# Attention weights split early and kept as fp16 in DRAM: a one-core Trainium2 decoder trunk

## The chip, the cores and the metric

The kernel runs on one core of a Trainium2 chip. The core has four compute engines: TensorE (PE, matrix products; PEld is its loading of weights), VectorE (DVE), ScalarE (ACT) and GpSimd (POOL). SyncE (SP) issues DMAs, as POOL and ACT also can. Each engine works through its own queue of instructions in the order in which the program was built, and waits at an instruction until the semaphores named there are reached. The metric is the device time of one execution in microseconds (us). Before the change it was 1152.69 us, the median of three runs (1151.28 to 1153.98).

## The reference: what is computed

The input x is 512 tokens of width 1024 in float32. Layer 0 is a gated short convolution and an MLP; then one shared key and value side is projected; layer 1 is native sparse attention (compressed, selected and window branches, 16 heads) and an MLP; a last RMS norm follows. Cut to what matters here:

```python
def short_conv_mixer(h, w_in, conv_w, w_out):
    b_gate, c_gate, u = jnp.split(h @ w_in, 3, axis=-1)
    v = c_gate * u
    vp = jnp.pad(v, ((0, 0), (CONV_WIDTH - 1, 0), (0, 0)))
    conv = sum(conv_w[k] * vp[:, k:k + S] for k in range(CONV_WIDTH))
    return (b_gate * conv) @ w_out

def squared_relu_mlp(h, w1, w2):           # 1024 -> 4096 -> 1024
    return jnp.square(jax.nn.relu(h @ w1)) @ w2

# layer 0:  x += short_conv_mixer(rms(x), ...);  x += squared_relu_mlp(rms(x), w1[0], w2[0])
# then:     kv = rms(x) @ w_kv   (six parts of 256); compress_blocks(k), compress_blocks(v)
#           with phi_k_w1, phi_k_w2, phi_v_w1, phi_v_w2
# layer 1:  q, gates = rms(x) @ b_w_qg;  o = three branches of attention;  x += o @ b_w_o
#           x += squared_relu_mlp(rms(x), w1[1], w2[1])
```

All weights arrive in float32.

## The kernel before

**Precision by splitting.** TensorE multiplies in fp16. A float32 operand is split into a high part (rounded to fp16) and a low part (the remainder, fp16), and a product of two operands is three matmuls: high by high, high by low, low by high (`mm3`, L338 to L341). The high part of a weight is made by ACT (L193), the low part by DVE (L194), which reads the float32 weight and the high part.

**The weight pieces.** All weights are listed in `pieces` in the order of their use. A usual piece is 128 x 1024 float32, 512 KB: half of the 1024 rows (4 blocks of 128) by 256 columns. A piece goes through three steps. `load_piece` brings it into one of three `wst` buffers by a DMA on SP's queue. `convert_piece` splits it into one of four `whi` and one of four `wlo` buffers (L193, L194). `next_piece` hands it to the matmuls. `ahead` converts two pieces ahead of use, `drain(ahead())` does it at once, and after a conversion the next loads are issued. Which of the four buffers a piece gets, and where an instruction stands in its engine's queue, is decided when the program is built, by a list scheduler of the framework.

**The stages**, with their times in the profile: the first stage, where the input projection a_w_in is multiplied pair by pair (0 to 140 us; pair 0 to 47); the mixer's output projection a_w_out (140 to 181); layer 0's MLP in two halves, each of 8 up pairs and then a down projection (up 181 to 266, down 266 to 345, up 345 to 424, down 424 to 503); the lead-in of attention with the first key and value parts (503 to 559); attention (559 to 797); layer 1's MLP (797 to the end). A "pair" is two blocks of 128 output features; it takes two pieces and 48 matmuls of 512 columns.

**One up pair** (`mlp_up`): 48 matmuls; then ml_t on DVE (L497, relu and scale, two instructions), ml_z on ACT (L499, the square), four sums of ml_z on POOL (L501, for the down projection, which is done in seven products of half-size blocks), rh on ACT (L502, high part), rl on DVE (L503, low part). The conversions of the next two pieces (L193, L194) stand in the same ACT and DVE queues. ml_t has one buffer, ml_z two. The down projections take rh and rl of all 8 pairs of the half (L548 to L550) and weights that are first summed on DVE (L180) and then split (L182, L183), with buffers of their own.

**Attention** uses 26 usual pieces and two small ones (phi_k_w2, phi_v_w2): parts of w_kv (4), phi_k_w1 (4), phi_v_w1 (4), parts of b_w_qg (6), and b_w_o (8). It interleaves many small tasks of softmax and selection with their conversions, which are done there in steps, mostly of 512 columns.

Of the kernel before, what the change touches and what calls it, by code (L numbers as in the profile page):

```python
# [22 lines left out]
SW = 256.0  # L23
# [25 lines left out]
def body(ctx, tc, x, rel_bias, norm_mix, norm_mlp, mlp_w1, mlp_w2, a_w_in, a_conv_w, a_w_out,  # L49
# [42 lines left out]
    def mlp_pieces(layer):  # L92

        for half in range(2):
            for p in range(8 * half, 8 * half + 8):
                up_pair(mlp_w1[layer], p)
            for p in range(4):
                down_blocks(mlp_w2[layer], p, half)

# [2 lines left out]
            cols(w, c0, 256, scale, k, 4)  # L102


    v = a_w_in[0].rearrange("(c p) (s n) -> c p s n", p=128, s=3)
    for c in range(8):
        pieces.append((v[c, :, :, 0:256], (3, 256), SW))
    for p in range(1, 4):
        for part in (1, 2, 0):
            block(a_w_in[0], part * D + p * 256)  # L110
    for p in range(4):
        block(a_w_out[0], p * 256)
    mlp_pieces(0)
    for part in (2, 4, 3, 5):
        block(w_kv, part * 256)
    cols(b_w_qg[0], 1024, 48, SW)
    block(b_w_qg[0], 0)
    block(w_kv, 0)
    block(b_w_qg[0], 256)
    block(phi_k_w1, 0, SW, 0, 16)  # L120
# [6 lines left out]
    for g in range(0, 4, 2):  # L127
        for p in range(4):
            cols(b_w_o[0], p * 256, 256, SW, 2 * g, 4)
    mlp_pieces(1)  # L130

    NS, NW, AHEAD, PIECE = 3, 4, 2, 1024
# [14 lines left out]
    def load_piece():  # L147
        i = pos["dma"]
        if i >= len(pieces):
            return  # L150
        src, shape, _ = pieces[i]
        if shape is None:
            t = wk[0].tile([128, PIECE2], F32, name="wst2", bufs=NS2)
            for k, u in enumerate(src):
                nc.sync.dma_start(t[:, k * PIECE:k * PIECE + 512].rearrange("p (j n) -> p j n", j=2), u)
        else:
            t = wpool.tile([128, PIECE], F32, name="wst", bufs=NS)
            a, n = shape
            v = t[:, :a * n].rearrange("p (a n) -> p a n", a=a)
            if len(src.shape) == 4:  # L160
                v = v.rearrange("p a (j n) -> p a j n", j=2)
                for j in range(2):
                    nc.sync.dma_start(v[:, :, j], src[:, :, j])
            else:
                nc.sync.dma_start(v, src)
        staged[i] = t
        pos["dma"] += 1

    def convert_piece(step=1024):

        i = pos["cv"]
        if i >= len(pieces):
            return
        _, shape, sc = pieces[i]
        t = staged.pop(i)
        pos["cv"] += 1
        if shape is None:
            b = t.rearrange("p (k b n) -> p k b n", k=2, n=128)
            for e, o, x, y in W_SUMS:
                DVE.tensor_tensor(b[:, :, o], b[:, :, x], b[:, :, y], op=e)  # L180
            hi, lo = (wk[0].tile([128, 2, 7, 128], F16, name=n, bufs=NW2) for n in ("whi2", "wlo2"))
            ACT.activation(hi, b[:, :, 1:], AF.Copy, scale=sc)  # L182
            DVE.scalar_tensor_tensor(lo, b[:, :, 1:], sc, hi, op0=OP.mult, op1=OP.subtract)  # L183
            ready[i] = (hi, lo)
            yield
        else:
            a, n = shape
            hi = wpool.tile([128, PIECE], F16, name="whi", bufs=NW)
            lo = wpool.tile([128, PIECE], F16, name="wlo", bufs=NW)
            for s in range(0, a * n, step):  # L190
                e = min(s + step, a * n)
                w = t[:, s:e]
                ACT.activation(hi[:, s:e], w, AF.Copy, scale=sc)  # L193
                DVE.scalar_tensor_tensor(lo[:, s:e], w, sc, hi[:, s:e], op0=OP.mult, op1=OP.subtract)  # L194
                yield
            r = lambda w: w[:, :a * n].rearrange("p (a n) -> p a n", a=a)
            ready[i] = (r(hi), r(lo))
        while pos["dma"] < len(pieces):
            like = [j for j in range(pos["cv"], pos["dma"]) if blocked(j) == blocked(pos["dma"])]
            if len(like) >= (NS2 if blocked(pos["dma"]) else NS):  # L200
                break
            load_piece()

    def next_piece():

# [183 lines left out]
    for p in range(4):  # L389
# [42 lines left out]
        for dst in (pc, pu, pb):  # L432
            if p:
                dst += [acc(), acc()]
                pair(xs, dst)
            else:
                for k in range(2):
                    first_pairs(dst, ws[k], 6 + k)
            drain(ahead())
            for m in range(2):  # L440
                ch = 2 * p + m
                if dst is pc:
                    if m == 0:
# [27 lines left out]
    for p in range(4):  # L471
        po = [acc(), acc()]
        pair(ys, po)
        if p < 3:
            drain(ahead())
        for m in range(2):
            residual_in(po[m], 2 * p + m, 1.0 / (SY * SW))
            ss.add(X[:, 2 * p + m])
        for m in range(2):
            split_gain(xs, 2 * p + m, X[:, 2 * p + m], "mlp0")  # L480
        drain(ahead())
    first.__exit__(None, None, None)


    def mlp_up(xs, ss, rh, half, rb):
        turn[0] = 1
        for p in range(8):
# [3 lines left out]
            if first:  # L491
                pr = broadcast_rows(ss.r)
                rb = row_tile(pr, math.sqrt(SR) / (SW * SX))
            drain(ahead())
            t = wk[0].tile([128, 2, S], F32, name="ml_t", bufs=1)
            for m in range(2):
                DVE.scalar_tensor_tensor(t[:, m], ph[m], 0.0, rb, op0=OP.max, op1=OP.mult)  # L497
# [741 lines left out]
```

## Time and profile before

| | |
|---|---|
| median of three runs | 1152.69 us |
| the profiled execution, its own time | 1151.28 us |
| its span in the trace | 1149.5 us |
| TensorE busy | 1106.0 us |
| VectorE busy | 837.8 us |
| ScalarE busy | 582.7 us |
| GpSimd busy | 162.2 us |
| DMA, moved in all | 115.76 MB, mean 101 GB/s |
| granted TensorE clock | 0.994 |
| L193 (high parts) | 171 instructions, 142.2 us |
| L194 (low parts) | 171 instructions, 168.1 us |

An instruction's row in the timeline gives its start in us from the start of the span, its duration, engine, line, operation and output<-inputs with sizes; "x2" at its end means that two were joined; in brackets stand the idle time of the engine before it and what ended that idle time. A row of the DMA issues gives the transfer, the queue (SPq, POOLq, ACTq), the count, the size of each and the median time from issue to landing. A row of the chain of waits gives start, duration, engine, tile and line of a step of the chain that ended last.

### The profile page before, as it was taken

The numbers are of one execution on the slowest core, as the hardware profiler recorded it, in microseconds if no ns is written. First come the engines' busy times: TensorE is split into PE (matmuls) and PEld (weight loads), VectorE is DVE, ScalarE is ACT, GpSimd is POOL, SyncE is SP. The second block draws the span as 40 slices with busy tenths as digits, with TensorE's granted clock in tenths as the row PEclk, the third lists the DMA queues.
The fourth block names the chain that finished last, engine by engine and source line by source line (L and its number), as shares of the span: only waits on it lengthen the run. The fifth ranks groups of instructions, "written<-read, shape, count | busy, mean of one in ns | idle before, by whom it ended". The sixth has DMA issues, their size and how long they took to land.

```text
span 1149.5 us, 20386 instructions
## 1 busy us (share of the span) xinstructions
PE 1106.0 (96%) x7959; PEld 694.1 (60%) x7959; DVE 837.8 (73%) x1604; ACT 582.7 (51%) x983; POOL 162.2 (14%) x211
## 2 busy tenths in 40 slices
PE   9999999999999999999999899999999999999996
PEld 4444444447884458868466665765444688445885
DVE  4755557765897557988487898997985588754795
ACT  4523235345333444457679778676644534343452
POOL 0000000422000220000120023111132200022031
PEclk9999999999999999999999999999999999999998
DMA  6433235433433333314333530111643343330231
GB/s 208 130 92 110 92 111 174 119 93 93 127 98 108 109 110 107 97 55 122 110 79 99 143 94 19 57 38 38 186 126 99 88 126 110 104 99 19 75 92 74
DMA packets 149379, 115.76 MB, mean 101 GB/s; under 512 B 8612, under 2 KB 146564, under 8 KB 149284
## 3 DMA queue, kind: packets, MB, share of 16 engines
q1 hardware_dynamic: 146736, 109.47, 31.8%
q10 hardware_dynamic: 2260, 4.40, 1.3%
q8 instruction: 62, 1.02, 0.4%
q0 software_dynamic: 288, 0.61, 0.2%
q14 instruction: 33, 0.27, 0.1%
HBM read 110.22 MB, written 2.14 MB: 98 GB/s over the span
## 4 chain that ended last, share of the span: by engine, by line
PE 49%; DVE 20%; ACT 12%; issue 8%; POOL 6%; DMA 4%; SPq 0%; DVEq 0%; ACTq 0%; POOLq 0%
POOL ml_z L501 6%; PE a L340 4%; PE a L339 4%; PE a L341 4%; DVE wlo L183 4%; DMA wst<-mlp_w_dram 4%; ACT rh L502 3%; PE b L339 3%; PE b L340 3%; PE b L341 3%; PE c L341 3%; PE c L339 3%; PE c L340 3%; DVE wst L180 3%; DVE wlo L194 3%
## 5 line engine op out<-in xcount | busy, mean ns | idle before, releaser
L193 ACT ACTIVATE whi<-wst 128x1024 f16<-128x1024 f32 (+2 forms) x171 | 142.2, 857 | 128.3 <-PE b L340 40.0
L194 DVE SCALAR_TENSOR_TENSOR wlo<-wst,whi 128x1024 f16<-128x1024 f32 (+2 forms) x171 | 168.1, 990 | 47.3 <-ACT whi L193 47.1
L501 POOL TENSOR_TENSOR ml_z<-ml_z 128x256 f32<-128x256 f32 x128 | 101.1, 811 | 604.5 <-ACT ml_z L499 403.9
L182 ACT ACTIVATE whi<-wst 128x1792 f16<-128x1792 f32 x64 | 107.0, 1692 | 132.6 <-DVE wst L180 107.8
L341 PEld LDWEIGHTS <-wlo 128*128 128x128 f16 x1024 | 100.1, 98 | 109.3 <-DVE wlo L194 0.7
L339 PEld LDWEIGHTS <-whi 128*128 128x128 f16 x1024 | 100.4, 98 | 108.1 <-issue 3.7
L503 DVE TENSOR_TENSOR rl<-ml_z,rh 128x1792 f16<-128x1792 f32 x32 | 64.8, 2025 | 136.9 <-ACT rh L502 136.9
L340 PEld LDWEIGHTS <-whi 128*128 128x128 f16 x1024 | 100.2, 98 | 105.0 <-issue 1.7
L183 DVE SCALAR_TENSOR_TENSOR wlo<-wst,whi 128x1792 f16<-128x1792 f32 x64 | 129.8, 2033 | 3.6 <-ACT whi L182 3.6
L180 DVE TENSOR_TENSOR wst<-wst 128x256 f32<-128x256 f32 x256 | 105.9, 455 | 24.1 <-DMA wst<-mlp_w_dram 23.1
L502 ACT ACTIVATE rh<-ml_z 128x1792 f16<-128x1792 f32 x32 | 54.3, 1697 | 103.4 <-POOL ml_z L501 103.4
L550 PEld LDWEIGHTS <-wlo 128*128 128x128 f16 x896 | 88.1, 98 | 16.6 <-issue 5.1
L549 PEld LDWEIGHTS <-whi 128*128 128x128 f16 x896 | 88.1, 98 | 14.8 <-issue 3.9
L548 PEld LDWEIGHTS <-whi 128*128 128x128 f16 x896 | 88.2, 98 | 11.0
L499 ACT ACTIVATE ml_z<-ml_t 128x1024 f32<-128x1024 f32 x32 | 33.8, 1057 | 90.5 <-DVE ml_t L497 90.5
L341 PE MATMUL b<-xsh,wlo 128*128 128x512 f16 x208 | 78.8, 379 | 0.0
L340 PE MATMUL b<-xsl,whi 128*128 128x512 f16 x208 | 78.8, 379 | 0.0
L339 PE MATMUL b<-xsh,whi 128*128 128x512 f16 x208 | 78.7, 379 | 0.0
L922 ACT ACTIVATE at_p<-at_s,at_m 128x128 f32<-128x128 f32 (+3 forms) x128 | 71.3, 557 | 13.4 <-DVE at_m L919 13.0
L549 PE MATMUL a<-rl,whi 128*128 128x256 f16 x256 | 70.3, 275 | 4.6 <-DVE rl L503 4.6
L339 PE MATMUL c<-xsh,whi 128*128 128x512 f16 x192 | 72.8, 379 | 0.0
L340 PE MATMUL c<-xsl,whi 128*128 128x512 f16 x192 | 72.8, 379 | 0.0
(312 smaller groups left out, 2757.5 us busy)
## 6 DMA issues: line engine op xcount, KB each, us to landing
wst<-mlp_w_dram SPq DMA_DIRECT2D x256, 256.0 KB, 3.4
wst<-a_w_in_dram SPq DMA_DIRECT2D x18, 512.0 KB, 3.6
wst<-w_kv_dram SPq DMA_DIRECT2D x12, 512.0 KB, 3.7
T<-ext_d ACTq DMA_DIRECT2D x4, 1056.0 KB, 6.0
wst<-a_w_out_dram SPq DMA_DIRECT2D x8, 512.0 KB, 3.5
wst<-b_w_qg_dram SPq DMA_DIRECT2D x8, 512.0 KB, 4.3
wst<-b_w_o_dram SPq DMA_DIRECT2D x8, 512.0 KB, 3.5
wst<-a_w_in_dram SPq DMA_DIRECT2D x8, 384.0 KB, 5.5
```

Source lines behind the costliest of these rows:

```text
L180: DVE.tensor_tensor(b[:, :, o], b[:, :, x], b[:, :, y], op=e)
L182: ACT.activation(hi, b[:, :, 1:], AF.Copy, scale=sc)
L183: DVE.scalar_tensor_tensor(lo, b[:, :, 1:], sc, hi, op0=OP.mult, op1=OP.subtract)
L193: ACT.activation(hi[:, s:e], w, AF.Copy, scale=sc)
L194: DVE.scalar_tensor_tensor(lo[:, s:e], w, sc, hi[:, s:e], op0=OP.mult, op1=OP.subtract)
L339: PE.matmul(ps, w[0], xs[0], start=start, stop=False)
L340: PE.matmul(ps, w[0], xs[1], start=False, stop=False)
L341: PE.matmul(ps, w[1], xs[0], start=False, stop=stop)
L501: POOL.tensor_tensor(z[:, o], z[:, a], z[:, b], op=e)
L502: ACT.activation(rh[0][:, p], z[:, 1:8], AF.Copy)
L548: PE.matmul(acc7[i], wh, xh, start=c == 0 and not other, stop=False, skip_group_check=other)
L549: PE.matmul(acc7[i], wh, xl, start=False, stop=False, skip_group_check=other)
```

## The change

Of attention's 28 pieces, the 26 of full size are taken out of attention's conversions. Behind each part of pairs 1 to 3 of the first stage (9), each pair of a_w_out (4) and the first 13 up pairs of layer 0 (8 in the first half, 5 in the second), one of them is added to the list of pieces (`spare_piece`). It goes through load and conversion like any other, in the same rings of three `wst` and four `whi` and `wlo` buffers. When its turn comes, `store_piece` takes it and writes its two fp16 parts to DRAM (`kept`), by two DMAs of 256 KB on GpSimd's queue; then it converts ahead as usual. In attention the piece is loaded by two DMAs on SP's queue directly into a `whi` and a `wlo` buffer, and not converted. The two small pieces are treated as before. In the program built, L193 and L194 with 171 instructions each become 147 each; GpSimd issues 58 DMAs in place of 6, and SP 415 in place of 363. The matmuls are the same.

```diff
         for half in range(2):
             for p in range(8 * half, 8 * half + 8):
                 up_pair(mlp_w1[layer], p)
+                if layer == 0:
+                    spare_piece()
...
+    late = pieces[:]
+    pieces.clear()
+    spare = [k for k, (_, shape, _) in enumerate(late) if shape[0] * shape[1] == 1024]
+    stores, loads, kept = {}, {}, {}
+
+    def spare_piece():
+        if spare:
+            stores[len(pieces)] = spare[0]
+            pieces.append(late[spare.pop(0)])
...
+    for p in range(1, 4):
+        for part in (1, 2, 0):
+            block(a_w_in[0], part * D + p * 256)
+            spare_piece()
+    for p in range(4):
+        block(a_w_out[0], p * 256)
+        spare_piece()
+    mlp_pieces(0)
...
+    for k, (src, shape, sc) in enumerate(late):
+        if shape[0] * shape[1] == 1024:
+            loads[len(pieces)] = k
+        pieces.append((src, shape, sc))
...
-        if shape is None:
+        if i in loads:
+            t = []
+            for name, d in zip(("whi", "wlo"), kept[loads[i]]):
+                w = wpool.tile([128, PIECE], F16, name=name, bufs=NW)
+                nc.sync.dma_start(w, d)
+                t.append(w.rearrange("p (a n) -> p a n", a=shape[0]))
+        elif shape is None:
...
-        if shape is None:
+        if i in loads:
+            ready[i] = tuple(t)
+        elif shape is None:
...
+            if i in loads:
+                full = i >= pos["use"] + NW - 1
+            else:
+                like = [j for j in range(pos["cv"], i) if j not in loads and blocked(j) == blocked(i)]
+                full = len(like) >= (NS2 if blocked(i) else NS)
+            if full:
+                break
             load_piece()
+
+    def store_piece():
+        i = pos["use"]
+        if i not in stores:
+            return
+        kept[stores[i]] = [dram.tile([128, PIECE], F16, name=f"kept{i}{m}") for m in "hl"]
+        for d, w in zip(kept[stores[i]], next_piece()):
+            nc.gpsimd.dma_start(d, w.rearrange("p a n -> p (a n)"))
+        drain(ahead())
...
         drain(ahead())
+        store_piece()
...
             drain(ahead())
+            store_piece()
             t = wk[0].tile([128, 2, S], F32, name="ml_t", bufs=1)
```

More of the change, by code (lines that the diff above doesn't have):

```diff
@@ L102, in block @@
             cols(w, c0, 256, scale, k, 4)
[L105 to L117, printed above, removed]
     block(w_kv, 0)
@@ L129, in body @@
             cols(b_w_o[0], p * 256, 256, SW, 2 * g, 4)
+    late = pieces[:]
[6 more added lines that the diff above has]
+            pieces.append(late[spare.pop(0)])
+    v = a_w_in[0].rearrange("(c p) (s n) -> c p s n", p=128, s=3)
+    for c in range(8):
+        pieces.append((v[c, :, :, 0:256], (3, 256), SW))
+    for p in range(1, 4):
[6 more added lines that the diff above has]
+    mlp_pieces(0)
+    for part in (2, 4, 3, 5):
+        block(w_kv, part * 256)
+    cols(b_w_qg[0], 1024, 48, SW)
+    block(b_w_qg[0], 0)
+    for k, (src, shape, sc) in enumerate(late):
+        if shape[0] * shape[1] == 1024:
+            loads[len(pieces)] = k
+        pieces.append((src, shape, sc))
+    assert not spare
     mlp_pieces(1)
@@ L198, in convert_piece @@
         while pos["dma"] < len(pieces):
-            like = [j for j in range(pos["cv"], pos["dma"]) if blocked(j) == blocked(pos["dma"])]
-            if len(like) >= (NS2 if blocked(pos["dma"]) else NS):
+            i = pos["dma"]
+            if i in loads:
[4 more added lines that the diff above has]
+            if full:
                 break
             load_piece()
+    def store_piece():
[6 more added lines that the diff above has]
+        drain(ahead())
     def next_piece():
@@ L494, in mlp_up @@
             drain(ahead())
+            store_piece()
             t = wk[0].tile([128, 2, S], F32, name="ml_t", bufs=1)
```

## The prediction

> **What bounds the kernel now.** I read the page's busy line first, then the windows (busy time by stage), then the timeline of the up projections engine by engine, because the change puts its additions there, then the chain of waits inside attention, where it takes work away.
>
> ```profile
> span 1149.5 us, 20386 instructions
> PE 1106.0 (96%) x7959; PEld 694.1 (60%) x7959; DVE 837.8 (73%) x1604; ACT 582.7 (51%) x983; POOL 162.2 (14%) x211
> ```
>
> PE leaves 43.5 us of the span idle, so nothing off PE can gain more than that. The windows show where. Columns: window, its length, then busy time (instructions) of PE, PE's weight loads, DVE, ACT, POOL, the granted clock, the DMA share and GB/s.
>
> ```profile
> 47.00:140.00 93.00, 93.00 (x433) 42.08 (x431) 51.25 (x71) 26.29 (x33) 0.00 (x0) 1.00 0.36 108
> 140.00:181.00 41.00, 41.00 (x191) 18.58 (x190) 24.01 (x32) 16.54 (x22) 0.00 (x0) 1.00 0.33 101
> 181.00:266.00 85.00, 83.65 (x394) 38.57 (x393) 60.96 (x76) 40.71 (x37) 22.42 (x24) 1.00 0.43 125
> 345.00:424.00 79.00, 79.00 (x368) 35.79 (x366) 49.07 (x61) 32.67 (x29) 16.92 (x24) 1.00 0.35 105
> 559.00:797.00 238.00, 219.59 (x2339) 148.67 (x2340) 202.10 (x671) 181.65 (x521) 44.12 (x59) 1.00 0.25 71
> ```
>
> They are, in order: the first stage (pairs 1 to 3), the output projection of the mixer, the layer-0 up projections (first half, second half), and attention. PE is full in the first two and in the second half of the up projections; attention has 238.00 - 219.59 = 18.4 us idle. By this table the up projections have DVE and ACT to spare, and a conversion more would cost nothing. The timeline says something else: it shows an order. One cycle of the second half:
>
> ```profile
> 362.77 0.38 PE L339 MATMUL a<-xsh,whi 128*128 128x512 f16 x1
> 373.13 0.38 PE L339 MATMUL b<-xsh,whi 128*128 128x512 f16 x1
> ...
> 361.90 1.28 DVE L497 SCALAR_TENSOR_TENSOR ml_t<-b,rb 128x512 f32<-128x512 f32 x2
> 363.21 1.06 ACT L499 ACTIVATE ml_z<-ml_t 128x1024 f32<-128x1024 f32 x1 [9.76 <-DVE ml_t L497]
> 364.35 2.90 POOL L501 TENSOR_TENSOR ml_z<-ml_z 128x256 f32<-128x256 f32 x4 [83.34 <-ACT ml_z L499]
> 367.29 1.70 ACT L502 ACTIVATE rh<-ml_z 128x1792 f16<-128x1792 f32 x1 [3.02 <-POOL ml_z L501]
> 368.89 1.99 ACT L193 ACTIVATE whi<-wst 128x1024 f16<-128x1024 f32 x2
> 369.01 2.02 DVE L503 TENSOR_TENSOR rl<-ml_z,rh 128x1792 f16<-128x1792 f32 x1 [4.70 <-ACT rh L502]
> 370.95 1.22 DVE L194 SCALAR_TENSOR_TENSOR wlo<-wst,whi 128x1024 f16<-128x1024 f32 x1
> 372.09 1.28 DVE L497 SCALAR_TENSOR_TENSOR ml_t<-c,rb 128x512 f32<-128x512 f32 x2
> 373.40 1.06 ACT L499 ACTIVATE ml_z<-ml_t 128x1024 f32<-128x1024 f32 x1 [2.53 <-DVE ml_t L497]
> ```
>
> PE's pairs start 373.13 - 362.77 = 10.36 us apart. Beside them runs a ring through three queues that work strictly in order: the square (L499), four sums on POOL, rh (L502), rl on DVE, one low-part conversion (L194), the next ml_t, the next square. Its period is 373.40 - 363.21 = 10.19 us, only 0.17 below PE's. The low part that DVE ends at 370.95 + 1.22 = 372.17 is needed by PE's pair at 373.13, so the ring has one lead of 1.0 us and then nothing. ACT's own leg (square, sums, rh, two conversions) leaves it idle 2.53 us.
>
> **The change, part by part.** (a) 26 pieces of attention's weights are converted during the first stage (9), the mixer's output projection (4) and 13 of the 16 layer-0 up pairs, one behind each pair, in the same four whi/wlo buffers. (b) Each is written to DRAM by two DMAs of 256 KB on POOL's queue. (c) Attention loads the fp16 pieces with two SP DMAs of 256 KB in place of one of 512 KB, and has no conversions for them.
>
> *(a) and (b) in the up projections.* In the changed program ACT's order behind rh is: the high part of the stored piece S; the high part of the next piece F, which is placed in the buffer of S and so waits until the store of S has landed; the high part of the other next piece, G; and only then the next square. Let x be a store's time from issue to landing. ACT's leg is then 4.08 (367.29 - 363.21) + 1.60 (368.89 - 367.29) + 1.00 (S, half of 1.99) + x + 1.99 (F and G) = 8.67 + x. Call it cycle A. In other cycles (B) the low part of F, which waits for the store of the low part, stands in DVE's queue between the two halves of the next ml_t: 5.68 to the start of rl, 3.20 for rl and S's low part (369.01 to 372.17, and 0.04), x, 1.22 for F, 0.64 for the second half of ml_t, 0.10 to the square: 10.84 + x. Read from the order in the program, the cycles with a store between pairs are, in the first half, pairs 1-2 A, 2-3 A, 3-4 B, 4-5 A, 5-6 B, 6-7 A, and in the second half a B place at its first pair, then 8-9 A, 9-10 B, 10-11 A. Pairs 13 to 15 have no store.
>
> What x is, the trace of before shows only from other transfers:
>
> ```profile
> rb<-final_norm_dram POOLq DMA_DIRECT2D x2, 256.0 KB, 3.7
> out_dram<-xsh SPq DMA_DIRECT2D x2, 512.0 KB, 3.0
> big<-kr_hl SPq DMA_DIRECT2D x8, 7.8 KB, 1.9
> pe_in<-cmp_pe_v_dram POOLq DMA_DIRECT2D x1, 8.0 KB, 4.8
> ```
>
> The same queue and size took 3.7 us (a load); a store of twice the size on another queue took 3.0; the shortest row of all is 1.9, and a small one on POOL's queue took 4.8. I take 3.7, the row that shares queue and size, and keep 1.9 and 4.8 for the range. With 3.7, A is 12.4 and B is 14.5; over PE's 10.36 that is 2.0 and 4.2. In the first half the early cycles were already longer:
>
> ```profile
> 200.58 1.04 ACT L499 ACTIVATE ml_z<-ml_t 128x1024 f32<-128x1024 f32 x1
> 212.42 1.06 ACT L499 ACTIVATE ml_z<-ml_t 128x1024 f32<-128x1024 f32 x1 [0.76 <-DVE ml_t L497]
> 225.46 1.06 ACT L499 ACTIVATE ml_z<-ml_t 128x1024 f32<-128x1024 f32 x1 [3.20 <-DVE ml_t L497]
> 236.23 1.06 ACT L499 ACTIVATE ml_z<-ml_t 128x1024 f32<-128x1024 f32 x1 [2.53 <-DVE ml_t L497]
> ```
>
> Pairs 1-2 took 13.04 (225.46 - 212.42), which covers A: 0. Pairs 2-3 took 10.77: 12.4 - 10.77 = 1.6. Then 4.2 + 2.0 + 4.2 + 2.0 = 12.4. First half: 14.0; PE already waits in this half (83.65 of 85), so I give it no lead. Second half: at its first pair F's low part starts when the store has landed, 11.1 us after PE's start of the pair (5.2 until half the pair frees the buffer, 1.0 and 1.2 for the two conversions, 3.7 for x), and the square comes 1.22 + 0.64 + 0.10 later, at 13.0, against 10.36 + 1.28 = 11.6 before: 1.4; then 2.0 + 4.2 + 2.0, less the lead of 1.0: 8.6. Together +22.6. With x = 1.9: 5.2 and 3.0, +8.2. With x = 4.8: 19.9 and 12.9, +32.8.
>
> [...]
>
> When this leg is late, PE waits next at the ends of the halves, where the down projections take rl; before, that wait is small:
>
> ```profile
> PE a L549 <- DVE rl L503: 4.6, 3, 1.8
> ```
>
> *(a) and (b) before the up projections: 0.* There is no ring there; PE is full, DVE is busy 51.25 of 93 us and 24.01 of 41, ACT 26.29 and 16.54. A stored piece adds 1.0 to ACT and 1.2 to DVE for each pair of about 10 us, 13 times. F must wait for the store as well: buffer free, 1.0 + 1.2, 3.7, 2.2 for F, about 8 us, and PE needs F 15.5 us (a pair and a half) after the buffer came free. If that cover of some 7 us were gone, each such pair would cost what is lacking. DMA moves 108 GB/s at a share of 0.36; one piece in three more, read and written, takes it to about 0.7.
>
> POOL issues 52 DMAs. The row nearest to one is
>
> ```profile
> L1107 POOL DMA_DIRECT2D rb<-final_norm_dram x2 | 1.1, 568 | 0.0
> ```
>
> so 52 x 0.57 = 30 us on an engine that is busy 14%: the two issues end 1.1 us after the stored piece is converted, well ahead of POOL's next sums. Cost 0; between 0 and 13 x 1.1 = 14 if every pair's sums waited for them, which the order excludes, since they follow the square that itself waits.
>
> *(c) in attention: -7.7.* The conversions taken away there:
>
> ```profile
> 559.00:797.00 238.00, 27.38 (x45) 1.00 0.25 71
> 559.00:797.00 238.00, 32.19 (x45) 1.00 0.25 71
> ```
>
> (ACT's L193 and DVE's L194; the two small phi pieces remain.) On the chain of waits in this window stand 12 rows of these lines, from
>
> ```profile
> 572.22 0.64 ACT whi L193
> ...
> 782.00 0.56 DVE wlo L194
> ```
>
> which sum to 7.7 us. That is what I take. The lower end is 0 (the next item in the queues takes the place), the upper end PE's whole idle time, 18.4. The 26 loads become 52 SP DMAs of the same total bytes (two of 256 KB fp16 for 512 KB f32); a load is issued when its buffer comes free, three pieces ahead, with a DMA share of 0.25: 0. SP has nothing else queued that attention waits for.
>
> *Sum.* +22.6 - 7.7 = +14.9. The profiled execution took 1151.28 us (span 1149.5 and 1.78 around it): 1166.2. The median shown, 1152.69, lies 1.41 above it: 1167.6.
>
> **The rivals.** *Faster.* Stores land soon and attention gains all its idle time. At x = 2.4 (between 1.9 and 3.0) A is 11.1, B 13.2, the loss 12.0, and with 18.4 from attention the time is 1146.3; it decides for faster as soon as x is under 3.2 with 18.4, or under 1.8 with 7.7. For it: the freed 27.38 and 32.19 us lie on engines that are busy 182 and 202 of 238 us in attention, the one stage where PE waits most. Against it: only 12 of 90 such rows are on the chain, and no POOL row is under 3.6.
>
> *No net change.* x near 1.9 with the 7.7: +8.2 - 7.7, 1153.2.
>
> *Heavier.* The change doesn't do what it says: attention's chain is held by softmax and selection, the conversions only filled gaps, and nothing comes back, while stores take 4.8: 1152.69 + 32.8 = 1185.5. For it: POOL's 24 sums took 22.42 us in the half where DVE is busiest and 16.92 in the other, so POOL and DVE slow each other, and the stored pieces bring DVE's two-input conversions into that place. A conversion on DVE beside POOL shows the same from the other side:
>
> ```profile
> 713.79 1.26 DVE L194 SCALAR_TENSOR_TENSOR wlo<-wst,whi 128x512 f16<-128x512 f32 x1
> 717.12 0.69 DVE L194 SCALAR_TENSOR_TENSOR wlo<-wst,whi 128x512 f16<-128x512 f32 x1
> ```
>
> [...]
>
> **How the numbers follow.** The ring with x from 3 to 4.8 and 5 to 11 back from attention: 0.62, 1160 to 1181, at 1167.6. Faster: 0.14, 1140 to 1150. Near no change, up to 1155: 0.07, of which 0.04 within 0.2% (2.3 us, about what a measurement of this kernel tells from nothing). Heavier: 0.17, up to 1186. So faster 0.14, same 0.04, slower 0.82. The range 1151 to 1186 leaves out the faster cases and the tail above.
>
> **What would show it.** Right: squares in the layer-0 up projections 12 to 14.5 us apart while pairs carry a store, and 10.2 to 10.4 in the last three; ACT's and DVE's idle time there ended by POOL's store DMAs; PE's wait for rl at the ends of the halves several times 4.6 us in all; POOL's store rows near 3.7; attention 5 to 11 us shorter than 238; the windows up to 181 us unchanged. Wrong: stores landing under 2 us or squares still about 10.4 apart (then the loss is gone); PE idle before 181 us (the cover of 7 us was not there); attention shorter by far more than 8 or not at all.

## The result: 52 us slower, and the profile after

The changed kernel takes 1204.92 us (median of 6 runs, 1202.08 to 1208.44), the kernel before 1153.04 (6 runs, 1150.12 to 1157.04): a ratio of 1.0455, 95% interval 1.0433 to 1.0477. The direction was as forecast. The size, +51.9 us, is more than three times the +14.9 of the sum, and the time lies above the range. The profiled execution of the changed kernel took 1208.09 us.

The first lines are of the changed kernel's page, the last one is the same group of the kernel before:

```profile
span 1206.3 us, 20550 instructions
PE 1122.1 (93%) x7959; PEld 697.5 (58%) x7959; DVE 840.0 (70%) x1580; ACT 584.0 (48%) x959; POOL 194.0 (16%) x263
...
L223 DVE SCALAR_TENSOR_TENSOR wlo<-wst,whi 128x1024 f16<-128x1024 f32 (+3 forms) x147 | 164.9, 1128 | 110.2 <-issue 46.5
...
L194 DVE SCALAR_TENSOR_TENSOR wlo<-wst,whi 128x1024 f16<-128x1024 f32 (+2 forms) x171 | 168.1, 990 | 47.3 <-ACT whi L193 47.1
```

VectorE and ScalarE are hardly busier than before (837.8 and 582.7 us). What grew is waiting: VectorE stood idle 110.2 us ahead of the low-part conversions (47.3 before). The windows by stage, cut where TensorE's same matmul starts (first stage, output projection, up and down of the first half, up of the second half, attention; columns as in the prediction):

```profile
47.00:143.00 96.00, 93.47 (x434) 42.04 (x432) 52.70 (x70) 32.57 (x38) 9.13 (x17) 1.00 0.60 185
143.00:195.50 52.50, 43.58 (x192) 18.98 (x191) 31.27 (x39) 20.80 (x27) 4.32 (x8) 0.90 0.53 166
195.50:304.30 108.80, 91.23 (x394) 39.69 (x393) 73.94 (x88) 48.61 (x46) 34.59 (x39) 0.91 0.59 178
304.30:393.70 89.40, 80.40 (x692) 68.57 (x691) 64.44 (x97) 34.26 (x26) 8.24 (x11) 0.96 0.38 116
393.70:488.20 94.50, 83.73 (x368) 36.14 (x367) 56.32 (x69) 37.45 (x33) 22.56 (x32) 0.96 0.44 134
623.20:855.60 232.40, 217.82 (x2341) 149.16 (x2342) 177.99 (x628) 160.98 (x477) 43.00 (x58) 1.00 0.25 75
```

| stage | before, us | after, us | difference | forecast |
|---|---|---|---|---|
| first stage, pairs 1 to 3 | 92.9 | 95.8 | +2.9 | 0 |
| mixer's output projection | 41.0 | 52.5 | +11.5 | 0 |
| up, first half | 85.1 | 108.9 | +23.8 | +14.0 |
| down, first half | 79.0 | 89.3 | +10.4 | 0 |
| up, second half | 79.0 | 94.5 | +15.5 | +8.6 |
| attention | 237.8 | 232.4 | -5.4 | -7.7 |
| all the rest | | | -1.9 | 0 |

The differences come from unrounded times and add up to the +56.8 between the two profiled executions. Three places show how a store turns into time on TensorE. The first stands at the start of the mixer's output projection:

```profile
150.18 0.54 POOL L245 DMA_DIRECT2D kept37l<-wlo  x1 [2.66 <-DVE wlo L223]
...
154.98 1.23 DVE L223 SCALAR_TENSOR_TENSOR wlo<-wst,whi 128x1024 f16<-128x1024 f32 x1 [5.09 <-issue]
...
156.12 0.68 DVE L507 TENSOR_TENSOR cv_b<-c,rb 128x512 f32<-128x512 f32 x1
...
158.04 1.23 ACT L404 ACTIVATE yh<-cv_b 128x512 f16<-128x512 f32 x2 [5.58 <-DVE cv_b L508]
...
158.72 0.59 PE L383 MATMUL a<-yh,whi 128*128 128x512 f16 x1 [7.37 <-ACT yh L404]
```

The low part of a stored piece goes out at 150.18 and lands 4.7 us later. VectorE's next instruction puts the next piece into the same buffer and waits for that (the profile shows the wait as "issue"). cv_b, the last channels of the first stage, stands behind it in VectorE's queue, yh waits for cv_b, and TensorE waits 7.37 us for yh. The second is a cycle of the kind that the prediction called B, at the end of the first half:

```profile
294.81 1.04 ACT L546 ACTIVATE ml_z<-ml_t 128x1024 f32<-128x1024 f32 x1
...
304.53 0.68 DVE L544 SCALAR_TENSOR_TENSOR ml_t<-b,rb 128x512 f32<-128x512 f32 x1
...
304.91 0.54 POOL L245 DMA_DIRECT2D kept70l<-wlo  x1 [1.69 <-DVE wlo L223]
...
310.90 1.22 DVE L223 SCALAR_TENSOR_TENSOR wlo<-wst,whi 128x1024 f16<-128x1024 f32 x1 [5.68 <-issue]
...
312.04 0.68 DVE L544 SCALAR_TENSOR_TENSOR ml_t<-b,rb 128x512 f32<-128x512 f32 x1
...
312.76 1.06 ACT L546 ACTIVATE ml_z<-ml_t 128x1024 f32<-128x1024 f32 x1 [5.72 <-DVE ml_t L544]
...
312.78 0.37 PE L595 MATMUL b<-rh,whi 128*128 128x256 f16 x1 [5.44 <-DVE ml_t L544]
```

The squares ahead of it show a B cycle of 16.43 us and an A cycle of 11.28:

```profile
267.10 1.06 ACT L546 ACTIVATE ml_z<-ml_t 128x1024 f32<-128x1024 f32 x1
...
283.53 1.06 ACT L546 ACTIVATE ml_z<-ml_t 128x1024 f32<-128x1024 f32 x1 [4.00 <-DVE ml_t L544]
...
289.19 1.04 ACT L222 ACTIVATE whi<-wst 128x1024 f16<-128x1024 f32 x1
292.90 2.00 ACT L222 ACTIVATE whi<-wst 128x1024 f16<-128x1024 f32 x2 [2.67 <-DVE wlo L223]
294.81 1.04 ACT L546 ACTIVATE ml_z<-ml_t 128x1024 f32<-128x1024 f32 x1
```

In the A cycle ScalarE makes the stored high part at 289.19, stands still for 2.67 us and makes the two next high parts; the square follows them without a gap. The store of the high part is issued at 290.53 and lands 2.3 us later, just before 292.90; the low part that the row names was done 0.4 us earlier (291.26 + 1.22 us, by VectorE's rows). In the B cycle, as forecast, the waiting low part stands between the two halves of ml_t. Not forecast: TensorE's first matmuls of the down projection need the accumulator that the second half of ml_t has yet to read, so they wait 5.44 us too. The third is TensorE itself, behind a wait of 8.8 us in the first up pair (windows of TensorE alone: busy time, granted clock, DMA share, GB/s):

```profile
201.00:206.00 5.00, 0.00 (x0) 0.57 0.59 199
206.00:211.00 5.00, 4.39 (x11) 0.50 0.83 228
211.00:216.00 5.00, 5.00 (x27) 0.90 0.94 294
```

After the wait the granted clock is 0.50 for some 5 us. In the four stages from the output projection to the second up half, TensorE is busy longer for the same matmuls: by 2.6 us in the output projection, 7.6 and 4.7 in the two up halves, and 3.0 in the first down projection, where it was 77.44 before:

```profile
266.00:345.00 79.00, 77.44 (x692) 67.51 (x690) 63.45 (x98) 32.20 (x24) 5.64 (x8) 1.00 0.37 109
```

So some 18 of the 61 us by which these four stages grew are TensorE being busy longer, and the other 43 are waits. In the stretches of these stages with a granted clock of 0.50 TensorE is busy 29.7 us; by an estimate, half of that, the clock accounts for about 15 of the 18; the other 3 were not traced to a cause.

### The profile page after: what moved, and what is told of

It reads as the page before. It is cut to its first block, busy times and chain, and to the rows that moved or that the text cites. A ratio compares the mean times of both kernels' runs of the same rounds, so it can differ in the third digit from the quotient of the medians.

```text
span 1206.3 us, 20550 instructions
## 1 busy us (share of the span) xinstructions
PE 1122.1 (93%) x7959; PEld 697.5 (58%) x7959; DVE 840.0 (70%) x1580; ACT 584.0 (48%) x959; POOL 194.0 (16%) x263
## 4 chain that ended last, share of the span: by engine, by line
DVE 19%; PE 17%; ACT 10%; issue 7%; POOL 6%; DMA 3%; SPq 1%; DVEq 0%; ACTq 0%; POOLq 0%
POOL ml_z L548 5%; DVE wlo L212 4%; ACT rh L549 3%; DMA wst<-mlp_w_dram 3%; DVE wst L209 3%; DVE ml_t L544 2%; DVE wlo L223 2%; ACT ml_z L546 2%; PE a L383 2%; PE c L975 2%; PE a L385 2%; PE a L384 2%; DVE X L562 1%; ACT at_p L969 1%; DVE at_pl L981 1%
## 5 line engine op out<-in xcount | busy, mean ns | idle before, releaser
L223 DVE SCALAR_TENSOR_TENSOR wlo<-wst,whi 128x1024 f16<-128x1024 f32 (+3 forms) x147 | 164.9, 1128 | 110.2 <-issue 46.5
L222 ACT ACTIVATE whi<-wst 128x1024 f16<-128x1024 f32 (+3 forms) x147 | 137.3, 963 | 124.1 <-DVE wlo L223 23.8
L548 POOL TENSOR_TENSOR ml_z<-ml_z 128x256 f32<-128x256 f32 x128 | 107.3, 857 | 314.7 <-ACT ml_z L546 303.7
L212 DVE SCALAR_TENSOR_TENSOR wlo<-wst,whi 128x1792 f16<-128x1792 f32 x64 | 129.9, 2035 | 3.6 <-ACT whi L211 3.6
L385 PE MATMUL c<-xsh,wlo 128*128 128x512 f16 x192 | 74.4, 388 | 6.2 <-DVE wlo L223 6.1
L966 DVE CUSTOM_DVE_ANT_0 at_s<-b,T 128x128 f32<-128x128 f32 (+3 forms) x128 | 61.0, 482 | 27.2 <-PE b L962 15.4
```

What stands on the lines that cost most here:

```text
L385: PE.matmul(ps, w[1], xs[0], start=False, stop=stop)
L548: POOL.tensor_tensor(z[:, o], z[:, a], z[:, b], op=e)
```

## The experiments

Three explanations were put to the test. Theory 1 is the wait of the in-order queues for a store's landing. Theory 2 is the added work itself. Theory 3 is GpSimd: its DMA issues, and its sums. All runs were timed beside the kernel before, which took 1152.04 to 1153.68.

### A buffer of its own for the stored piece

```diff
+            wp, nm, nb = (wk[0], "s", 1) if i in stores else (wpool, "w", NW)
-            hi = wpool.tile([128, PIECE], F16, name="whi", bufs=NW)
-            lo = wpool.tile([128, PIECE], F16, name="wlo", bufs=NW)
+            hi = wp.tile([128, PIECE], F16, name=nm + "hi", bufs=nb)
+            lo = wp.tile([128, PIECE], F16, name=nm + "lo", bufs=nb)
```

> The stored pieces are converted into a high and a low buffer of their own (one of each); work, stores and loads are the same. Theory 1 (what costs is the wait for a store to land, in the in-order queues of ScalarE and VectorE, because the next piece is put into the buffer just stored): the waits go, 1146 to 1153 us. Theory 2 (the added conversions and transfers themselves overload the stages): still 1185 or more. Theory 3 (GpSimd's DMA issues and the slower sums on GpSimd): 1160 to 1175.

1163.77 us, ratio 1.0099 (1.0075 to 1.0124): 41.1 of the 51.9 us are gone, with the same conversions, stores and loads. The output projection is at 41.0 us again and the second up half at 79.0. The first up half keeps 5.6 us, its down projection 7.0. So the shared buffer carries four fifths, and something else some 10 us and the gain of attention on top. Not all of the four fifths is the landing of stores, as theory 1 has it: the runs without stores below show that sharing costs 10.4 us even then. The own buffer is also a fifth one, and no run gave the shared ring a fifth; the run with stores on SyncE's queue below gets most of the time back with four.

### Which of the two parts: low or high alone

```diff
-            lo = wpool.tile([128, PIECE], F16, name="wlo", bufs=NW)
+            lo = wk[0].tile([128, PIECE], F16, name="slo", bufs=1) if i in stores else \
+                wpool.tile([128, PIECE], F16, name="wlo", bufs=NW)
```

> The changed kernel with a buffer of its own for the stored low part only; the next piece's high part still goes into the stored piece's high buffer and waits for that store (2.3 to 5.3 us). If the wait for the low part's store on VectorE is what costs (where the products of the stage end, ml_t, cv_b and the residual, stand behind it): 1163 to 1172 us, nearly as with both buffers. If the wait for the high part on ScalarE carries the loss, as the prediction had it in most cycles: 1185 or more.

> The counterpart: a buffer of its own for the stored high part only; low parts share and wait for the low store (4.2 to 6.2 us). If the low part's wait is the cause: the first stage and the mixer's output projection still lose 10 us or more, and the whole takes 1185 to 1205. If the high part's wait is the cause: 1163 to 1172.

With the low part's own buffer 1173.98 us, with the high part's 1194.16. Against the changed kernel that is 30.9 and 10.8 us less; together 41.7, as both buffers gave (41.1). The windows of the output projection and the two up halves, first with the low part's own buffer, then with the high part's:

```profile
139.10:180.10 41.00, 41.00 (x192) 18.57 (x191) 26.90 (x35) 19.74 (x25) 3.78 (x7) 1.00 0.65 197
180.10:280.10 100.00, 88.14 (x395) 38.63 (x394) 68.69 (x83) 46.41 (x43) 32.36 (x38) 0.97 0.62 183
...
366.10:449.20 83.10, 79.85 (x368) 35.44 (x367) 51.55 (x62) 35.69 (x31) 21.25 (x32) 1.00 0.48 145
```

```profile
142.00:193.90 51.90, 43.29 (x192) 18.88 (x190) 31.14 (x40) 21.83 (x28) 4.32 (x8) 0.90 0.55 169
193.90:289.40 95.50, 85.79 (x394) 38.66 (x393) 73.75 (x87) 50.49 (x48) 36.02 (x39) 0.98 0.68 203
...
378.00:469.90 91.90, 81.96 (x368) 35.92 (x367) 54.56 (x66) 35.96 (x33) 21.50 (x31) 0.96 0.45 134
```

Three quarters of what the two buffers save is the low part's, on VectorE. The high part's, on which the forecast laid most of its cycles, is the smaller one in the whole. In the first up half it is the larger one: that stage took 108.9 us, 100.0 with the low part's own buffer and 95.5 with the high part's.

### Stores on SyncE's queue

```diff
-            nc.gpsimd.dma_start(d, w.rearrange("p a n -> p (a n)"))
+            nc.sync.dma_start(d, w.rearrange("p a n -> p (a n)"))
```

> The changed kernel with the stores issued on SyncE's queue in place of GpSimd's. If the store's landing is what costs, and it is slow because GpSimd issues it (low parts 4.5 to 6.2 us), landings of about 3 us (the 512 KB stores on this queue took 3.0) shorten the longest cycles from 16.5 and 18 us to about 14 and the time to 1185 to 1197. If GpSimd's issues and sums are the cost (theory 3): about 1165 to 1180. If the weight loads queued behind a store on SyncE are late: 1205 or more.

1171.04 us, 33.9 less than the changed kernel, but not by the way that was expected. On the whole the stores land no sooner: the low parts mostly take 4.0 to 6.1 us here and 4.2 to 6.2 in the changed kernel. Rows of the DMA issues in this run, and behind them two of the changed kernel:

```profile
kept25l<-wlo SPq DMA_DIRECT2D x1, 256.0 KB, 5.5
kept58l<-wlo SPq DMA_DIRECT2D x1, 256.0 KB, 5.8
```

```profile
kept25l<-wlo POOLq DMA_DIRECT2D x1, 256.0 KB, 6.2
kept58l<-wlo POOLq DMA_DIRECT2D x1, 256.0 KB, 4.4
```

What differs is the program that was built. Ahead of the up projections 12 low parts waited 1.8 to 6.6 us for a store's landing in the changed kernel; here one does, 3.0 us, while ScalarE's high parts still wait there, up to 5.8 us. So the next low part mostly gets another buffer, and the high part alone still follows the stored piece into its own. In the up projections eight low parts still wait, 1.6 to 2.5 us each. That is nearly the run with the low part's own buffer, and the times are 2.9 us apart. The first stage and the output projection lose nothing (92.9 and 41.0).

```diff
+            wp, nm, nb = (wk[0], "s", 1) if i in stores else (wpool, "w", NW)
...
-            nc.gpsimd.dma_start(d, w.rearrange("p a n -> p (a n)"))
+            nc.sync.dma_start(d, w.rearrange("p a n -> p (a n)"))
```

> Both parts in their own buffer, stores on SyncE's queue: against the own-buffer run it takes away only GpSimd's issuing of stores. If the issues on GpSimd (2 x 0.54 us per piece, in front of its sums) lengthen the first half's cycles (16.1, 14.4, 13.8 us): 3 to 6 us less than that run's 1163.8, 1157 to 1161. If the sums are slow because VectorE's conversions run beside them: unchanged, 1162 to 1165.

With own buffers the queue makes no difference: 1164.98 us against 1163.77. GpSimd's busy time in the first up half falls from 39.30 to 22.38 us and the stage only from 90.7 to 89.1. So issuing on GpSimd falls as a cause of the time; the forecast priced it at 0, and that holds. The other part of theory 3, slower sums, is not settled by this run: in the first four pairs the sums still take 4.2 to 4.3 us in place of 2.9 (before, the first three took 5.6, 5.1 and 3.5).

### Conversions without stores

```diff
-            loads[len(pieces)] = k
+            pass
...
-        kept[stores[i]] = [dram.tile([128, PIECE], F16, name=f"kept{i}{m}") for m in "hl"]
-        for d, w in zip(kept[stores[i]], next_piece()):
-            nc.gpsimd.dma_start(d, w.rearrange("p a n -> p (a n)"))
+        next_piece()
```

> The 26 pieces are loaded and converted early as in the change, but not stored, and attention converts its weights itself as before. Theory 1: 1153 to 1158 us, since 1.0 us on ScalarE and 1.2 us on VectorE per pair fit when no store is waited for. Theory 2: 1190 or more, nearly all of the loss. Theory 3: 1153 to 1158 as well.

> As the run that only converts early, with the stored pieces' own buffer; nothing is stored, and attention converts its weights itself. If the 12.5 us cycles of that run come from the shared buffer (the next piece's high part waits until the low part of the dropped piece is made from the same buffer), they fall to 11.3, which is 10.2 and one more low part of 1.14 on VectorE, and the second half loses nothing: 1163 to 1168 us. If the work alone fills the engines: 1175 as before. If the stores of the own-buffer run cost something by themselves (GpSimd's sums took up to 7.7 us there instead of 2.9), this run's first half of the up projections is shorter than 90.7 us, by about 3.

1174.95 us, and 1164.57 with own buffers. Converting early is not free: with the shared buffer it costs about 22 us, without one store, and 10.4 of them go with own buffers. A cycle of the first of these runs:

```profile
265.88 1.06 ACT L544 ACTIVATE ml_z<-ml_t 128x1024 f32<-128x1024 f32 x1 [1.54 <-DVE ml_t L542]
...
271.54 1.04 ACT L222 ACTIVATE whi<-wst 128x1024 f16<-128x1024 f32 x1
...
271.66 2.03 DVE L548 TENSOR_TENSOR rl<-ml_z,rh 128x1792 f16<-128x1792 f32 x1 [4.68 <-ACT rh L547]
...
273.60 1.22 DVE L223 SCALAR_TENSOR_TENSOR wlo<-wst,whi 128x1024 f16<-128x1024 f32 x1
...
274.86 2.00 ACT L222 ACTIVATE whi<-wst 128x1024 f16<-128x1024 f32 x2 [2.28 <-DVE wlo L223]
...
278.40 1.06 ACT L544 ACTIVATE ml_z<-ml_t 128x1024 f32<-128x1024 f32 x1 [1.54 <-DVE ml_t L542]
```

It takes 278.40 - 265.88 = 12.52 us. ScalarE makes the early piece's high part at 271.54, and the next high part goes into the same buffer: it waits 2.28 us until VectorE has made the low part, which reads that buffer, and VectorE comes to it only behind rl. With own buffers the same cycles take 11.33 (285.72 - 274.39):

```profile
274.39 1.06 ACT L545 ACTIVATE ml_z<-ml_t 128x1024 f32<-128x1024 f32 x1 [2.72 <-DVE ml_t L543]
...
285.72 1.06 ACT L545 ACTIVATE ml_z<-ml_t 128x1024 f32<-128x1024 f32 x1 [2.72 <-DVE ml_t L543]
```

That is the ring's 10.19 and 1.14 more, one more low part between rl and ml_t (1.14 is the step from one low part to the next instruction, 370.95 to 372.09 in the prediction's rows); TensorE's pair of 10.36 us is passed by 0.97. The own-buffer run's first up half and its down projection lose 3.4 and 6.5 us, and the second up half, with two such cycles, nothing. Another 3.6 of its 12.5 us lie in attention (241.4 us in place of 237.8), for which no cause was found.

> Own buffers and stores on SyncE, and the stored piece is no longer converted ahead, so that in the program built its low part stands in front of rl (in the time in which VectorE waits for the sums) in the cycles to the 3rd, 4th pair, and behind rl, in front of ml_t, in the later cycles with a store. If the ring is what the conversions alone cost: near 10.2 to 10.8 us where it stands in front of rl and 11.3 where it stands behind; 1158 to 1164 in all. If the cost is the work as such, or GpSimd's sums beside it: all cycles with a stored piece 11.3 or longer.

```diff
-        while pos["cv"] < len(pieces) and pos["cv"] < pos["use"] + (AHEAD2 if blocked(pos["cv"]) else AHEAD):
+        while pos["cv"] < len(pieces) and pos["cv"] not in stores and pos["cv"] < pos["use"] + (AHEAD2 if blocked(pos["cv"]) else AHEAD):
...
-            store_piece()
             t = wk[0].tile([128, 2, S], F32, name="ml_t", bufs=1)
...
             DVE.tensor_tensor(rh[1][:, p], z[:, 1:8], rh[0][:, p], op=OP.subtract)
+            store_piece()
```

1162.30 us. This run did not tell its two cases apart: in the cycles with the low part ahead of rl, low parts of the down projection (L212, 2.02 us) stand in the ring as well, and GpSimd's four sums take 4.27 us beside VectorE's work in place of 2.90; these cycles took 13.5 to 13.7 us, the others 11.3 to 11.7.

```diff
-                if layer == 0:
-                    spare_piece()
+            if layer == 0 and (c // 2) % 2 == 1 and not (p == 3 and c % 8 == 6):
+                spare_piece()
...
-        spare_piece()
+        if p < 3:
+            spare_piece()
...
+                store_piece()
```

> All 26 pieces, stores on SyncE's queue, but none in the up projections: 9 in the first stage, 3 in the mixer's output projection, 7 in each down projection of layer 0 (behind every second blocked piece), where no square, sum and high part wait for one another. If the ring of the up projections is what the early conversions cost, the up stages take 85 and 79 us again with 10.2 us cycles, the down stages lose 0 to 3 each, and attention gives 3 to 6 back: 1147 to 1153 us. If the work itself costs wherever it stands: the down stages lose 7 or more each, 1160 or more.

1175.75 us, ratio 1.0186 (1.0161 to 1.0212). The up stages took 84.9 and 79.3 us, but the down stages lost 13.5 and 14.3. The scheduler converts the first stored pieces of a down projection in the last up pairs, where one cycle now takes 17.3 us (ScalarE waits 5.4 us there for a store and VectorE 3.3) and the first product then waits 6.9 us for rh. So the waits were moved, not removed, and whether the same work is free away from the ring stays open.

### What attention gains

```diff
-            loads[len(pieces)] = k
+            pass
```

> Early conversions and stores as in the change, but attention does not use what was stored and converts its weights itself. All theories leave the early loss; the difference to the changed kernel is what attention gains. If its 5.4 us shorter window (and 1.7 us behind it) comes from the conversions taken away: 1210 to 1213 us. If it comes from elsewhere: 1205.

```diff
-            stores[len(pieces)] = spare[0]
-            pieces.append(late[spare.pop(0)])
+            if len(spare) == 26:
+                stores[len(pieces)] = spare[0]
+                pieces.append(late[spare[0]])
+            spare.pop(0)
...
-        for name, d in zip(("whi", "wlo"), kept[loads[i]]):
+        for name, d in zip(("whi", "wlo"), kept[0]):
```

> One piece is converted and stored early, behind the first part of pair 1; attention loads this one piece 26 times in place of its own weights, so its output is not the reference's: 25 conversions ahead of attention and their stores are left out. If attention's gain is its own: 1145 to 1148 us. If it needs the early stages' delay: 1153.

1215.62 us, 10.7 above the changed kernel, and 1146.36, ratio 0.9941 (0.9919 to 0.9963), 6.7 below the kernel before. These are two readings of attention's gain, and the forecast 7.7 lies between them. With the run that only converts, the first of them splits the change in three: conversions +21.9 us, stores +40.7 (1174.95 to 1215.62), attention's loads -10.7. The gain does not come piece by piece, however:

```diff
-                if layer == 0:
-                    spare_piece()
...
-        if shape[0] * shape[1] == 1024:
+        if k in stores.values():
             loads[len(pieces)] = k
```

The second of the two runs also cuts `spare` to its last 13 entries (`[13:]`).

> Stores on SyncE's queue, buffers shared, and only the 13 pieces of the first stage and the mixer's output projection; the other 13 are converted in attention. In the run with SyncE's stores these two stages took exactly what they took before (92.9 and 41.0 us), and without stored pieces the up projections keep their 10.2 us cycles: no loss. Attention keeps half of its gain of 6.7 to 10.7 us: 1147 to 1150, faster than both kernels. If attention's gain hangs on the late pieces (b_w_o and the last b_w_qg): 1152 or more.

> As the run with 13 pieces and stores on SyncE, but the 13 pieces are the last of attention's list (the last part of phi_v, b_w_qg from 512 on, b_w_o) in place of the first 13, whose attention window stayed at 237.8 us. If attention's gain hangs on the late pieces, whose conversions stand beside softmax, it shows here: the window 4 to 6 us shorter, 1147 to 1150 us in all, faster than both kernels. If the gain needs all 26: again within 1 us of 238, 1152 to 1154.

1153.65 us, ratio 1.0013 (0.9999 to 1.0028), and 1152.95, ratio 0.9992 (0.9976 to 1.0008). In both the early stages up to 181 us lose nothing. The first up half, which has no stored piece, is 2.6 and 6.0 us longer: TensorE waits in its first pair for the scale of the norm, 2.2 and 3.5 us. Its down projection is 1.7 us shorter in both. In neither has attention gained:

```profile
557.90:795.70 237.80, 221.27 (x2340) 150.87 (x2341) 191.92 (x653) 172.53 (x502) 43.48 (x58) 0.99 0.26 73
```

```profile
562.00:799.80 237.80, 220.86 (x2339) 151.12 (x2340) 188.61 (x646) 170.55 (x495) 43.40 (x58) 0.99 0.25 71
```

The first 13 pieces save VectorE about 10 us there and the last 13 some 13 us, and the window stays at 237.8 with each; with all 26 it is 232 to 236 in the runs that had them. Why half of them give nothing was not found.

```diff
-                if layer == 0:
+                if layer == 0 and 8 <= p < 13:
...
             block(a_w_in[0], part * D + p * 256)
-            spare_piece()
+            if p > 1:
+                spare_piece()
```

> Own buffer, and only the 15 pieces whose places lost nothing in the own-buffer run: pairs 2 and 3 of the first stage (6), the mixer's output projection (4), the second half of the up projections (5); the other 11 are converted in attention as before. Theory 1 with the ring: the early stages take what they took before (140, 41, 85, 79, 79 us), and attention keeps 15 of 26 parts of its gain of 6.7 to 10.7 us: 1146 to 1150, faster than both. If any one more conversion costs (theory 2): 1156 or more.

1154.60 us, ratio 1.0026 (1.0009 to 1.0043): not faster. Attention is 2.8 us shorter, but two cycles at the end of the first half are 11.3 us, since the pieces of the second half are converted ahead there, and the down stages are 3.9 and 2.2 us longer. No version that does the whole work beats the kernel before; the two with 13 pieces equal it.

### The clock behind a wait

```diff
+            if c == 6 and fill:
+                for _ in range(fill):
+                    PE.matmul(ps[0], idle[:, 0:128], idle, start=False, stop=False)
...
-        pair(ys, po)
+        pair(ys, po, fill=30 if p == 0 else 0)
```

> The changed kernel with 30 matmuls of zeros (30 x 0.216 = 6.5 us) added into the accumulation where TensorE waits 7.4 us in the mixer's output projection; the sums are unchanged. If the half granted clock behind that wait comes from TensorE having stood still, the clock there stays at 1.00 and the stage of 52.5 us gets 2 to 2.7 us shorter although it has 30 matmuls more. If the clock has another cause: the same 52.5 or longer.

The stage takes 49.5 us in place of 52.5, with 30 matmuls more, and the whole 1202.58. TensorE's windows of the changed kernel over this stretch, then of this run:

```profile
155.00:159.00 4.00, 0.28 (x1) 0.50 0.38 129
159.00:163.00 4.00, 2.91 (x8) 0.50 0.52 177
```

```profile
155.00:159.00 4.00, 2.45 (x11) 1.00 0.57 185
159.00:163.00 4.00, 4.00 (x20) 1.00 0.84 271
```

So the half clock here comes from TensorE having stood still: behind 7.37 us of idling it was 0.50, and with the 30 matmuls in that place it stayed at 1.00. How long TensorE must stand still for that was not shown: a single wait of 2.60 us, in the second up half of the changed kernel, was followed by 0.50 as well (416.8 to 420.2). After the waits of 7.37 and 8.8 us the clock came back about 5.4 us after work had resumed.

## Why the prediction was wrong, point by point

- **Where the difference lies.** Between the profiled executions the change cost 56.8 us, 41.9 more than the sum. Of these, 14.4 lie before the up projections, 16.7 in them, 10.4 in the first down projection and 2.3 in attention; the rest gave 1.9 back.
- **The place was right, in part.** Squares in the up projections stand where it put them: the last three of the second half 10.2 us apart, those with stored pieces 11.3 to 17.9. Up projections and attention together were forecast at +14.9 and measured +33.9 (23.8 + 15.5 - 5.4).
- **"Before the up projections: 0" failed: +14.4.** The cover was reckoned for the piece that waits (7 us until TensorE needs it). What counted was what is queued behind it on VectorE: cv_b and the residual. This is the step that failed worst: the prediction named the instruction behind the wait in the up projections and not here. The run with the low part's own buffer takes this loss away whole (92.9 and 41.0 us).
- **"PE waits next at the ends of the halves" named the right place and gave it no price.** The first down projection lost 10.4. The wait for rl that it had in mind stayed at 5.1 us in all (4.6 before); what came up is the wait for the accumulator, 5.44 us. There the late pair ends up, and with it the half clock (0.50 from 313.0 to 317.5 us).
- **x was one number; it is two.** The high part's store landed in 2.3 to 5.3 us (2.3 in 9 of 13 in the up projections), the low part's, issued behind it, in 4.2 to 6.2 (the last one in 3.6), against 3.7 for both. For A the formula held, and only x was off: in three cycles ScalarE stands still for 2.67 us (the store's 2.3 and 0.3 until it is issued), 8.67 + 2.67 = 11.3, and 11.3 was measured; in the fourth it stands still for 4.77 us, 13.4 by the formula, and 13.4 was measured. The forecast was 12.4. In B cycles the forecast was 14.5, and 16.4, 17.9 and 16.5 were measured. The low part waited 4.6 to 6.3 us there in place of 3.7, and rl started 0.8 to 1.0 us later, since GpSimd's sums took 3.75 to 3.94 us in place of 2.90.
- **Small slips in the sums.** By the rows shown, rl starts 5.80 us behind the square, not 5.68, so B is 0.1 longer; and the sums for x = 1.9 and 2.4 (8.2 and 12.0) leave out the lead of 1.0 that the main sum takes off. Neither moves the forecast by much.
- **At x = 0 the formula gave no cost (8.67 under 10.36); that failed too.** It left out VectorE's leg of the ring where two low parts stand between rl and ml_t, 10.19 + 1.14, and the wait of the next high part for the low part made from the same buffer. That wait alone is 2.28 us in the run that only converts, so of the 2.67 us in the changed kernel's A cycles the store adds some 0.4. The two runs without stores show cycles of 11.3 us with own buffers and 12.5 with the shared one, and lose 12.5 and 21.9 us.
- **Early cycles of the first half.** Forecast 0 for pairs 1-2 and 1.6 for 2-3; measured 14.9 and 14.1 against 13.04 and 10.77, and 15.2 against 11.84 for the first. Conversions for the down projection stand in these cycles as well.
- **The clock was not in the sum.** About 15 us, as above; 43 are the waits themselves.
- **Attention: -7.7 forecast, -5.4 in the window.** The size is near by luck: by a sum of rows of the chain each half of the pieces should bring a part of the gain, and neither half alone brought any.
- **The heavier rival** had its time nearest (1185.5), for reasons that hold in part. Its 4.8 us are near what the low parts' stores took, and GpSimd's sums are slower, by some 1.0 us in a B cycle. Of the two conversions in its rows from the trace of before, the one of 1.26 us lies beside GpSimd's work (four instructions, 710.89 to 716.06), the one of 0.69 does not; no run tested that. But attention did give time back, and the losses before the up projections and in the first down projection are not in it.

## What to carry to other kernels

Before putting a store behind a buffer, ask which buffer the next user gets, and then read the whole in-order queue behind the instruction that will wait for the landing: its price was set here by the most urgent instruction queued there (cv_b, on whose account TensorE waited 7.37 us), not by when the waiting piece itself was needed. A buffer of its own for what is stored took away 41 of 52 us here without touching the work. An engine with idle time had little room here: VectorE was busy 49.07 of 79.00 us in the second up half before, but its instructions stood in a ring of 10.19 us beside TensorE's pairs of 10.36, and with one more low part of 1.14 us, in the run with own buffers and no stores, such a cycle took 11.33, 0.97 longer than a pair.

## What was not expected of the hardware

A wait of TensorE cost more than its length: after waits of 5.4 to 8.8 us the granted clock was 0.50 for 5.0 to 5.5 us of the work that followed, and 12 matmuls take 5.1 us there in place of 2.6. Of a piece's two stores of 256 KB, the second, mostly issued 1.3 to 3.4 us behind the first, took longer from its own issue to landing in nearly every pair, by up to 3.6 us on GpSimd's queue and 3.7 on SyncE's. One pair of the changed kernel:

```profile
kept70h<-whi POOLq DMA_DIRECT2D x1, 256.0 KB, 2.3
kept70l<-wlo POOLq DMA_DIRECT2D x1, 256.0 KB, 5.9
```

Why the second takes longer was not tested. GpSimd's four sums took 2.9 us while VectorE stood still, and up to 5.8 beside VectorE's conversions and sums of weights in the changed kernel (up to 5.6 in the first pairs of the kernel before). One of them:

```profile
254.09 5.51 POOL L548 TENSOR_TENSOR ml_z<-ml_z 128x256 f32<-128x256 f32 x4 [4.15 <-ACT ml_z L546]
```
